# Embedding lookup with added positions: first indices on the SyncE ring, first positions on the ScalarE ring

## Chip, cores and metric

One core of a Trainium2 chip. The metric is the device time of one execution in microseconds (us), lower is better. "Span" is the time from the first to the last instruction in the trace; it is some 5 us shorter than the device time.

In lines of the profile, DVE is VectorE, POOL GpSimd, ACT ScalarE and SP SyncE; a q behind the name is the engine's sequencer, which issues transfers and waits. A ring is the queue on which one engine's transfers reach the 16 transfer (DMA) engines. A load has landed when the last of its 16 semaphore increments has arrived. GpSimd's sequence of gathers is called its row.

## The reference

```python
def reference(indices, embedding_table, position_embed):
    token_embed = embedding_table[indices]          # indices (32, 512), table (50000, 512) float32
    return (token_embed + position_embed).astype(np.float32)   # positions (512, 512)
```

16,384 rows of 2 KB are gathered (33.6 MB), added to a position and stored (33.6 MB).

## The kernel before

Each of the 128 gathers brings 128 rows (256 KB) into a slot, GpSimd issues it, VectorE adds the positions, ScalarE issues the store. Before the gathers can start, the indices of the first batch must be in SBUF. That load and the first half of the positions are issued inside Tile's part of the program, which `tc.close()` and `tc.compile()` end with barriers across all engines (line 106); everything else comes after it.

```python
    def load(out, in_, done):
        return nc.scalar.dma_start(out=out, in_=in_).then_inc(done, 16)
    # ...
    for ins in (load(idx0[:, 0, :], idx_first[:, 0, :], s_first), load_pos(0)):
        tc.no_tile_sem_insts.add(ins.ins.name)
    tc.close()
    tc.compile()                       # barriers of all engines

    load(idx0[:, 1:, :], idx_first[:, 1:, :], s_next)      # the remaining indices of batches 1 to 3
    for j in range(J):
        load(idx_raw[j * B : (j + 1) * B, :], idx_rows[:, j, :], s_raw)
    load_pos(1)

    nc.gpsimd.wait_ge(s_first, 16)
    for g, (b, k) in enumerate(order):
        if g == half:                  # the third gather
            nc.gpsimd.wait_ge(s_next, 16)
        # ...
        ins = nc.gpsimd.indirect_dma_start(
            out=slots[b % SLOTS][:, k, :], out_offset=None, in_=table,
            in_offset=bass.IndirectOffsetOnAxis(ap=where, axis=0),
        ).then_inc(s_gather[g % LANES], 16)
    # ...
    # VectorE: copy of the positions to PSUM, then one add per gather
    # ScalarE: one store per add or pair of adds
```

## Time and profile before

| what | before |
|---|---|
| time, median of the first four runs | 179.29 us (178.99 to 179.32) |
| span | 173.3 us |
| GpSimd leaves Tile's barriers | 2.25 us |
| first indices landed (last of 16 increments) | 2.33 us |
| first gather starts | 3.13 us |
| step from gather to gather | 1.251 us |
| DMA rate from 40 us on | 410 to 419 GB/s |

The prediction below shows the lines that bound this kernel. Two more are from the timeline of the start; the columns are start, duration, engine, line, operation, and in brackets the idle time before it and what ended it. The first is VectorE's first copy of the positions, the second its second add:

```profile
4.64 0.69 DVE L145 COPY pos_ps<-pos_sb 128x512 f32<-128x512 f32 x1 [4.64 <-DMA pos_sb<-in_position_embed_dram]
...
10.28 0.69 DVE L150 TENSOR_TENSOR slot<-slot,pos_ps 128x512 f32<-128x512 f32 x1 [2.19 <-DMA slot<-in_embedding_table_dram,idx]
```

The copy waits for the positions alone, the add for the second gather's data.

### The profile page before, as it was taken

The page shows a single profiled execution, that of the slowest core. Times are in us where ns is not written, and L with a number is a line of the kernel's source. Part 1 is how long each engine was busy: PE and PEld are TensorE (multiplying, and loading weights), DVE is VectorE, ACT ScalarE, POOL GpSimd, SP SyncE. Part 2 cuts the span into 40 slices and gives each one's busy share as a digit, 9 for nine tenths or more (in the row PEclk, how much of TensorE's full clock was granted, in tenths as well). Part 3 has the DMA queues.
Part 4 walks back from the last instruction along what each step waited for, and adds up shares of the span by engine and source line. Part 5 has one row for each costly group of instructions (what it writes and reads, how often), then busy time and mean ns, then how long its engine had stood idle before and what let it go on. Part 6 is the DMA issues. An engine that isn't in the chain of part 4 may idle for free.

```text
span 173.3 us, 387 instructions
## 1 busy us (share of the span) xinstructions
DVE 90.7 (52%) x133; POOL 121.4 (70%) x132
## 2 busy tenths in 40 slices
DVE  0433855545555554555555555545555555546551
POOL 2777777777777777777777777777777777777400
DMA  4899999999999999999999999999999999999997
GB/s 128 242 324 331 345 392 365 415 409 412 411 415 402 407 421 419 409 421 420 420 416 421 420 417 419 422 416 420 421 419 417 421 419 418 419 422 415 420 420 308
DMA packets 21059, 68.34 MB, mean 394 GB/s; under 512 B 3776, under 2 KB 3904, under 8 KB 21056
## 3 DMA queue, kind: packets, MB, share of 16 engines
q10 hardware_dynamic: 10816, 34.76, 49.8%
q0 software_dynamic: 10240, 33.56, 49.7%
q14 instruction: 3, 0.02, 0.0%
HBM read 34.75 MB, written 33.55 MB: 394 GB/s over the span
## 4 chain that ended last, share of the span: by engine, by line
POOL 68%; issue 23%; DMA 5%; DVE 1%; POOLq 0%
POOL slot L128 68%; DMA slot<-in_embedding_table_dram,idx_t 4%; DVE slot L150 1%; DMA idx<-in_indices_dram 1%; POOLq L123 0%
## 5 line engine op out<-in xcount | busy, mean ns | idle before, releaser
L128 POOL DMA_INDIRECT slot<-in_embedding_table_dram,idx_t x112 | 105.9, 946 | 34.1 <-issue 34.1
L150 DVE TENSOR_TENSOR slot<-slot,pos_ps 128x512 f32<-128x512 f32 x128 | 87.9, 687 | 74.9 <-issue 46.1
L128 POOL DMA_INDIRECT slot<-in_embedding_table_dram,idx x16 | 15.3, 954 | 7.3 <-issue 4.6
L145 DVE COPY pos_ps<-pos_sb 128x512 f32<-128x512 f32 x4 | 2.8, 688 | 4.6 <-DMA pos_sb<-in_position_embed_dram 4.6
L140 DVE STREAM_TRANSPOSE idx_t<-idx_raw 128x128 int32<-128x128 int32 x1 | 0.4, 399 | 0.0
L186 POOL MEMSET const-float32-0.0<- 128x1 f32 x1 | 0.1, 98 | 0.2 <-issue 0.2
L186 POOL MEMSET const-uint8-127<- 128x1 uint8 x1 | 0.1, 118 | 0.0
L186 POOL MEMSET const-bfloat16-1.0<- 128x1 bf16 x1 | 0.1, 113 | 0.0
L186 POOL MEMSET const-float32-1.0<- 128x1 f32 x1 | 0.1, 104 | 0.0
## 6 DMA issues: line engine op xcount, KB each, us to landing
out_dram<-slot ACTq DMA_DIRECT2D x60, 512.0 KB
out_dram<-slot ACTq DMA_DIRECT2D x8, 256.0 KB
slot<-in_embedding_table_dram,idx_t POOLq DMA_INDIRECT x112
pos_sb<-in_position_embed_dram ACTq DMA_DIRECT2D x2, 512.0 KB, 4.6
slot<-in_embedding_table_dram,idx POOLq DMA_INDIRECT x16
idx_raw<-in_indices_dram ACTq DMA_DIRECT2D x4, 32.0 KB
idx<-in_indices_dram ACTq DMA_DIRECT2D x1, 4.0 KB, 1.6
idx<-in_indices_dram ACTq DMA_DIRECT2D x1, 12.0 KB
```

The source lines that it names most:

```text
L128: ins = nc.gpsimd.indirect_dma_start(out=slots[b % SLOTS][:, k, :], out_offset=None, in_=table, in_offset=bass.IndirectOffsetOnAxis(ap=whe ...
L140: nc.vector.transpose(out=idx_t[:], in_=idx_raw[:].rearrange("r (q k w) -> r k q w", k=K, w=2)[:, :, :, 0],)._wait_ge(s_raw, 16 * J).then_ ...
L145: nc.vector.tensor_copy(out=pos_ps[:, k, :], in_=pos_sb[:, k, :])._wait_ge(s_pos[k // half], 16).then_inc(s_ps, 1)
L150: nc.vector.tensor_tensor(out=part, in0=part, in1=pos_ps[:, k, :], op=add)._wait_ge(s_gather[g % LANES], rounds(g)).then_inc(s_add, 1)
L186: nc = _bacc.Bacc("TRN2", target_bir_lowering=False, num_devices=1)
```

## The change

ScalarE issues both early loads one after the other, which keeps it, and so the barrier, busy until 1.6 us. The change gives the index load to SyncE, so that the two issues run side by side.

```diff
-    def load(out, in_, done):
-        return nc.scalar.dma_start(out=out, in_=in_).then_inc(done, 16)
+    def load(out, in_, done, engine=nc.scalar):
+        return engine.dma_start(out=out, in_=in_).then_inc(done, 16)
 ...
-    for ins in (load(idx0[:, 0, :], idx_first[:, 0, :], s_first), load_pos(0)):
+    for ins in (
+        load(idx0[:, 0, :], idx_first[:, 0, :], s_first, engine=nc.sync),
+        load_pos(0),
+    ):
         tc.no_tile_sem_insts.add(ins.ins.name)
```

## The prediction

> **What bounds the kernel now.** I read the page first, then the waits, then the timeline of the first microseconds, the chain of waits (whole, and in windows at both ends), and last the DMA view of the first three microseconds.
>
> The page, parts 4 and 5:
>
> ```profile
> DVE 90.7 (52%) x133; POOL 121.4 (70%) x132
> POOL 68%; issue 23%; DMA 5%; DVE 1%; POOLq 0%
> L128 POOL DMA_INDIRECT slot<-in_embedding_table_dram,idx_t x112 | 105.9, 946 | 34.1 <-issue 34.1
> ```
>
> The chain that ended last is GpSimd: 128 gathers, each 946 ns of descriptor making, plus a gap "issue" before each. The list of waits says how large that gap is and whether the gathers ever wait for data:
>
> ```profile
> POOL slot L128 <- issue: 38.7, 127, 0.3
> POOL slot L128 <- DMA idx<-in_indices_dram: 2.7, 1, 2.7
> ```
>
> 127 gaps of 0.30 us, and one wait on data: the first gather's, for the first indices. So one gather comes every 0.946 + 0.305 = 1.25 us and nothing stops the row. The timeline has the first gather at 3.13 and the last at 162.06: 158.93 us for 127 steps, 1.2514 each. Each step brings 256 KB in and, later, sends 256 KB out: 524,288 B in 1.2514 us is 419 GB/s.
>
> The same figure is the DMA rate of the steady part, so the DMA could be the bound instead. Cutting the span into stretches gives:
>
> ```profile
> 12.00:14.00 2.00, 1.37 (x3) 1.68 (x2) 1.00 1.00 326
> 80.00:120.00 40.00, 21.84 (x32) 30.25 (x33) 1.00 1.03 419
> ```
>
> The fifth number on is the DMA share, then GB/s: the transfer engines are full from about 12 us. But pairing each gather with its add on the timeline (start to start) gives 3.7 us for the first gather, 5.8 for the second, 6.7 at the eleventh, 7.3 at the 30th and 7.4 at the 66th, the 102nd and the last. If the transfers were slower than GpSimd, this delay would keep growing by the difference at each step; it is flat from 40 us on. I therefore read GpSimd as the pacer and the DMA as just keeping up. The whole time is then a sum: first gather's start 3.13 + 127 x 1.2514 = 162.06; + 7.47 to its add = 169.54; + 0.69 for the add = 170.22; + some 3.0 for the last store and the clearing of semaphores = 173.3, the span. The timed runs have 179.27, so 6 us lie outside the span.
>
> Only the first term, 3.13, can be touched by this change. Its make-up, from the timeline and the chain in a window of the start:
>
> ```profile
> 0.74 0.38 ACTq L95 DMA_DIRECT2D idx<-in_indices_dram  x1
> 1.15 0.46 ACTq L95 DMA_DIRECT2D pos_sb<-in_position_embed_dram  x1
> 2.36 0.39 ACTq L95 DMA_DIRECT2D idx<-in_indices_dram  x1
> ```
>
> ```profile
> 0.74 1.60 DMA idx<-in_indices_dram
> 2.33 0.80 issue
> 3.13 1.08 POOL slot L128
> ```
>
> The indices are issued at 0.74, land at 2.33, and 0.80 us pass before the first gather shows. Beside this runs a second path: Tile closes its part with barriers (line 106) which all engines must reach. ACT reaches them only after its two issues:
>
> ```profile
> L106 ACTq DRAIN  x2: 8/80/151, 1.6 to 2.0; - x2
> ...
> L106 POOLq EVENT_SEMAPHORE  x2: 17/17/17, 2.2 to 2.2; - x2
> ```
>
> (the second line is the same line of source in the window from 2.1 to 3 us). In the record of single instructions ACT's drain starts at 1.645, GpSimd collects the five engines at 1.83, goes through a second round and leaves at 2.25, 0.08 us before the last of the sixteen index increments (2.33). So two paths reach the first gather almost together.
>
> **What the Trainium skill says.** "DMA: Bandwidth & Descriptors", section "Issuing engines are not separate DMA queues": transfers from all engines run on the same 16 DMA engines, and issuing from several saves only sequencer time. The trace has that time: 0.38 and 0.46 us on ACT's sequencer. The same page, "Queues, rings and completion order": SyncE and ScalarE own one ring each, each DMA engine takes turns between rings at packet granularity, and a semaphore increment lands only after every earlier write of that engine across its queues. The trace before has one hardware ring (q10) in use and can't show it. "Perfetto Trace Analysis", "DMA Instruction — HWDGE (DVE, Sync)": the descriptor generator is shared and is locked by one sequencer at a time. The trace before has no two issues at once, so doesn't show that either. The same page, "DMA Instruction — SWDGE (GPSIMD)": on GpSimd an instruction waits in a queue after decoding and the recorded time is that of the software that writes descriptors, so part of the 0.80 us is not in any record.
>
> **The change part by part.** Removed: ACT's first issue, 0.38 us plus the 0.03 to the next, 0.41 in all. Added: one issue on SyncE, which has nothing to do but the barrier. Moved: the positions' issue, from 1.15 to 0.74 (ACT leaves the opening barrier there).
>
> Step 1, the index landing. SyncE leaves the opening barrier 5 ns before ACT, so its issue starts at about 0.73 too. Same 0.38 issue, same 1.60 to landing: 2.33. The saving is nil, since the index load was already first on its own ring.
>
> Step 2, the positions. Before, they were issued at 1.15 and landed 3.5 later (the tile's own answer), and the first copy on VectorE began at 4.64. All 0.41 earlier: 4.23. VectorE's next step, the first add, waits for the first gather until 6.81, so the 0.41 us are idle time exchanged for idle time: 0.
>
> Step 3, the barrier. ACT's drain moves from 1.645 to about 1.23 (SyncE done at 0.73 + 0.38 = 1.11 is no later), hence GpSimd's exit from 2.25 to 1.84. The other loads on ACT (remaining indices, from 2.36) move to 1.95, the second positions from 4.73 to 4.32. The third gather needs the remaining indices only at 5.76, and they had landed by 4.73: 0.
>
> Step 4, contention. In the DMA view of the first 3 us (40 slices of 0.075 us), this row is the transfer engines' busy share:
>
> ```profile
> DMA  0000000000000000000000023300018934558999
> ```
>
> Index packets move from 1.73 to 2.0 and the first position packets from 2.24. Positions issued 0.41 earlier would start at 1.83, in the middle of the indices. Index packets took 9 ns each, position packets (4096 B) 159 ns at best and up to 0.69 us. Each engine has 8 index packets; as the engines' index completions are spread from 1.80 to 1.99 and the positions would sweep the engines in the same order about 0.1 behind, I estimate that most index packets stay ahead, and charge 0 to 0.4 us, 0.1 as the middle.
>
> Step 5, the 0.80. If it counts from the landing, the first gather moves to 3.13 + 0.1 = 3.23. If a part of it is GpSimd's own way from the barrier to the gather, it starts 0.41 earlier and the first gather can come as early as 2.72. VectorE's first copy came 0.02 after its last increment, and gathers with no wait follow in 0.30, so 0.80 after a landing is long; that speaks for the second. I give it one in three.
>
> Sum: 0.65 x (+0.1) + 0.35 x (-0.35) = -0.06 us. Everything after the first gather keeps its pace, so the time moves by the same: 179.27 - 0.06, about **179.2 us**.
>
> **Rivals.** (a) The barrier frees the first gather: 2.72 instead of 3.13, 178.9 us. For it: the odd 0.80 and the near tie of 2.25 and 2.33. Against it: the chain names the index DMA, and the landing itself isn't earlier. (b) The positions delay the indices: either ACT gets the generator first (the indices wait 0.4) or 4096 B packets stand between the 32 B ones, or a completion waits behind a position write. For it: the overlap worked out in step 4, which the old order on one ring avoided. Against it: SyncE is 5 ns ahead and its issue is 0.07 shorter. One to several packets of 0.16 to 0.5 us make +0.3 to +0.8: 179.6 to 180.1 us. (c) The DMA is the true bound and swallows a shift of GpSimd; then the earlier positions fill a hole in the transfers (their share is 0.72 from 4 to 6 us) and up to 0.3 us are won: 179.0. The flat 7.4 us speaks against it. (d) A second hardware ring costs something outside the span. No number here bears on it; I leave it a small chance of a microsecond or more.
>
> **Range and chances.** The first gather can move between -0.41 and about +0.8. The runs before lie between 178.99 and 179.32, so the median carries 0.2 either way. That makes 178.6 to 180.2; I cut the far end of (b) a little and take 178.5 to 180.0. Two per cent is 3.6 us, more than the whole 3.13 us that the change can touch going down, and four times the worst contention going up: within 2% at 0.98, one per cent each way.
>
> **What would show it.** Right: the issue of the indices on SyncE's queue at 0.73 to 0.76, positions on ACT's at 0.74; position landing near 4.2; the barrier on GpSimd ending at 1.8 to 1.9; gathers still every 1.25 us and 7.4 us to the add late in the run; the span moved by as much as the first gather's start. Step 1 is wrong if the indices land later than 2.5 (then b); step 5 is wrong if the first gather comes before 3.0 with the landing unmoved (then a). The pacer reading is wrong if the first gather's start moves and the end doesn't follow (then c), and if the span stays and the timed runs move, it is (d). The whole is wrong if the gathers' period changes: nothing here should do that.

## The result, and the profile after

The changed kernel took 178.51 us (median of four runs, 178.26 to 178.83); the kernel before 179.29 us in the same rounds. The ratio is 0.9962, 95% interval 0.9943 to 0.9981. Ratios in this document are the mean time of one kernel's fast runs over that of the other's of the same set, so not quite the ratio of the medians quoted. In all sets but this first one they come out of the listed runs only if the first run of each list is left out (that of the run under test is the profiled execution); means and differences in the text are over all listed runs.

The page of the changed kernel says that nothing happened to the bulk of the work (parts 4 and 5), and that 144 packets now go over a second hardware ring, q1 (part 3; packets, MB, share):

```profile
q10 hardware_dynamic: 10672, 34.75, 49.6%
q1 hardware_dynamic: 144, 0.00, 0.0%
...
POOL 65%; issue 25%; DMA 5%; DVE 3%
...
L131 POOL DMA_INDIRECT slot<-in_embedding_table_dram,idx_t x112 | 106.0, 947 | 34.1 <-issue 34.1
```

The list of waits of the changed kernel gives the same row of gathers: 127 gaps of 0.3 us and one wait on data at the start, 2.5 us now:

```profile
POOL slot L131 <- issue: 38.7, 127, 0.3
POOL slot L131 <- DMA idx<-in_indices_dram: 2.5, 1, 2.5
```

So the difference lies in the first microseconds. The timeline there:

```profile
0.74 0.40 ACTq L95 DMA_DIRECT2D pos_sb<-in_position_embed_dram  x1
0.74 0.37 SPq L95 DMA_DIRECT2D idx<-in_indices_dram  x1
1.90 0.40 ACTq L95 DMA_DIRECT2D idx<-in_indices_dram  x1
...
3.99 0.69 DVE L148 COPY pos_ps<-pos_sb 128x512 f32<-128x512 f32 x1 [3.99 <-DMA pos_sb<-in_position_embed_dram]
...
8.78 0.69 DVE L153 TENSOR_TENSOR slot<-slot,pos_ps 128x512 f32<-128x512 f32 x1 [0.80 <-DMA slot<-in_embedding_table_dram,idx]
```

The two issues are side by side at 0.74, ScalarE's next one comes at 1.90 instead of 2.36, the positions are there 0.65 us earlier, and the second add comes 1.5 us earlier. The chain of waits in the window from 0 to 9 us (start, duration, what):

```profile
0.74 1.97 DMA idx<-in_indices_dram
2.71 0.27 issue
2.98 1.08 POOL slot L131
```

Before it was 1.60, then 0.80, then the gather at 3.13. The indices now take 0.37 us longer to land, and yet the gather comes 0.15 us earlier, because the piece that follows the landing shrank from 0.80 to 0.27. GpSimd's last two steps of the barrier, in the window from 1.6 to 3 us, are earlier (2.2 before; count, ns, first and last start):

```profile
L109 POOLq EVENT_SEMAPHORE  x2: 17/17/17, 1.7 to 1.8; - x2
```

The second of them ends at 1.79, before at 2.25. The DMA view of the first 3 us shows why the landing is later. Each digit is the busy share of the transfer engines in 0.075 us:

```profile
DMA  0000000000000000000000029795499999949999
```

Before there was a hole between the indices (1.73 to 2.0 us) and the positions (from 2.24). Now the positions' packets begin at 1.81, while the last of the index packets are sent at 2.27 instead of 1.98, and the sixteen 4 B packets that make the load's increments start from 1.99 to 2.44 instead of 1.80 to 1.99 (both from the packet records of the traces).

That accounts for 0.15 us at the first gather, and even this isn't there at the end: the last gather of the two traces starts at the same 162.06 and both spans are 173.3 us. The other 0.6 us of the measured 0.78 is in none of these lines, so the first question was whether it is there at all.

### The profile page after: what moved, and what is told of

It reads as the page before. It is cut to its first block, busy times and chain, and to the rows that moved or that the text cites. A ratio compares the mean times of both kernels' runs of the same rounds, so it can differ in the third digit from the quotient of the medians.

```text
span 173.3 us, 387 instructions
## 1 busy us (share of the span) xinstructions
DVE 90.6 (52%) x133; POOL 121.5 (70%) x132
## 4 chain that ended last, share of the span: by engine, by line
POOL 65%; issue 25%; DMA 5%; DVE 3%
POOL slot L131 65%; DMA slot<-in_embedding_table_dram,idx_t 4%; DVE slot L153 3%; DMA idx<-in_indices_dram 1%
```

## The experiments

Two theories stood at the start. **T, two gates:** the first gather comes at the later of two times, a fixed time after GpSimd leaves the barrier, and 0.27 us after the indices land; the end follows GpSimd's row. **D:** something else wins, either the second ring outside the span, or the earlier transfers. A second question runs through all of them: does GpSimd's row set the end, or the transfers, which have no slack to see?

### after_again: the changed kernel once more

No edit. 

> The changed kernel once more, to size the 0.78 us. Theory T (two gates): the first gather comes at the later of barrier exit + up to 0.88 us and index landing + 0.27 us, and the rest of the kernel follows it; then the gain is the 0.15 us by which the first gather moved in the trace, ratio 0.9992, and the 0.9962 was mostly chance. Rival D (outside the span or another place): the ratio is again near 0.996 (0.994 to 0.998) while the first gather is only 0.15 us earlier.

Measured: 178.63 us against 178.56, ratio 1.000 (0.9969 to 1.003), first gather at 3.06 us. The 0.996 did not come back.

### before_again: the kernel before against itself

No edit. 

> The kernel before against itself: ratio 1.000. Both theories say the same; how far the ratio is from 1 says how small a difference the other runs can show. If it is off by more than 0.2%, differences of 0.2% are not to be explained.

Measured: 178.53 us, ratio 0.9993 (0.9967 to 1.002), first gather at 3.13. The half width of the interval is 0.27%, or 0.5 us: a difference of 0.15 us can be read in a trace, but not in these times. One source of the spread is visible: leaving out the first step, which is longer, the mean step from gather to gather was 1.2504 us in the first trace of this kernel and 1.2531 in this one, which makes 0.34 us over 126 steps.

### after_third: the changed kernel a third time

No edit. 

> The changed kernel a third time, to pool with the two earlier sets (ratios 0.9962 and 1.000). If there is a gain of the size of the first set, 0.994 to 0.998; if it is the 0.1 to 0.2 us of the first gather or nothing, 0.998 to 1.002.

Measured: 178.45 us against 178.54, ratio 0.9988 (0.9954 to 1.0023), first gather at 2.95. In the two repeats the means differ by 0.15 and 0.14 us (178.60 and 178.75; 178.42 and 178.56). In the first set the difference was 0.69, and most of it came from the other side: the four runs of the kernel before averaged 179.22, while its 11 runs in each later set averaged 178.75, 178.56 and 178.58. The changed kernel averaged 178.53, 178.60 and 178.42. Why the first four runs of before were slow isn't settled; the traced execution of that kernel took 177.92 us, 1.07 below the fastest of them. The gain in the repeats is of the order of the first gather's shift (0.07 and 0.18 us), but it hangs on single runs: without the first run of each list, as in the ratios, it is 0.01 and 0.21 us. Both intervals include 1, so a gain in time is not shown.

### idx_alone_act: only the indices in Tile's part, on the old ring

```diff
-    for ins in (load(idx0[:, 0, :], idx_first[:, 0, :], s_first), load_pos(0)):
+    for ins in (load(idx0[:, 0, :], idx_first[:, 0, :], s_first),):
         tc.no_tile_sem_insts.add(ins.ins.name)
     tc.close()
     tc.compile()
+    load_pos(0)
     load(idx0[:, 1:, :], idx_first[:, 1:, :], s_next)
```

> Only the first indices in Tile's part, on the ScalarE ring as before; the first positions right after the barrier, on the same ring. No second ring, no rival transfer for the indices. Theory T: barrier exit at about 1.7 us as in the changed kernel, indices landing at 2.33 as before, first gather at 2.33 + 0.27 = 2.60, so 0.53 before the kernel before, and the time 0.4 to 0.5 us below it (ratio 0.9975). If the 0.80 us counted from the landing instead, the first gather stays at 3.13. Rival D (the second ring or the early positions make the gain): ratio 1.000, since neither is there; positions land near 5.2 instead of 4.6.

Measured: 178.74 us, ratio 0.9987 (0.9954 to 1.0019). The landing is where it was (2.33), the barrier opens at 1.77 instead of 2.25, and the first gather comes at 2.65: the 0.80 us before it did not count from the landing. But the time did not move. The timeline of this run says what took the gain:

```profile
2.65 1.08 POOL L129 DMA_INDIRECT slot<-in_embedding_table_dram,idx  x1 [2.20 <-DMA idx<-in_indices_dram]
...
4.04 0.94 POOL L129 DMA_INDIRECT slot<-in_embedding_table_dram,idx  x1 [0.30 <-issue]
...
5.71 0.95 POOL L129 DMA_INDIRECT slot<-in_embedding_table_dram,idx  x1 [0.73 <-DMA idx<-in_indices_dram]
```

The third gather waits for the remaining indices, which now stand behind the positions: a step of 1.67 instead of 1.25 us, 0.42 of the 0.48 won. A new wait took the place of the old one, and I had not seen it coming.

### idx_alone_sp: the same on the SyncE ring

```diff
-    for ins in (load(idx0[:, 0, :], idx_first[:, 0, :], s_first),):
+    for ins in (load(idx0[:, 0, :], idx_first[:, 0, :], s_first, nc.sync),):
```

> As the run before, but the first indices go on the SyncE ring; positions again after the barrier. Theory T: the same first gather, about 2.60, and the same time as that run within 0.2 us. Rival D, if the second ring itself is worth something outside the span: 0.5 us or more below the run with the ScalarE ring, with the same span.

Measured: 178.95 us, ratio 1.0009 (0.9983 to 1.0035); landing 2.33, first gather 2.67, again a long third step (1.49 us). The second ring brings no gain by itself, and no cost that these runs could show: the device time minus the span was 5.2 us here and 5.0 with the old ring. The mean times of the two lie 0.42 us apart, not within the 0.2 that I expected, with overlapping intervals. In the trace, the adds lag behind the gathers by 8.1 us late in the run, against 7.6 with the old ring; this comes back below.

### rest_first: the new wait taken away

From the run before, with the remaining indices ahead of the positions:

```diff
     tc.compile()
-    load_pos(0)
     load(idx0[:, 1:, :], idx_first[:, 1:, :], s_next)
+    load_pos(0)
```

> As the run with the indices alone on the SyncE ring, but after the barrier the remaining indices go ahead of the first positions, so the third gather doesn't have to wait for them. First gather at about 2.65, steps of 1.25 us from there with no long one, so the last gather some 0.45 us before the kernel before's. If GpSimd's row alone sets the end, the time is 0.4 us below before (ratio 0.9975). If the transfers decide, then the later positions (landing near 5.5 instead of 4.6) take back what the earlier gather gives: first add not before 6.8, delay from gather to add near 8 instead of 7.4 in the steady part, ratio 1.000 within 0.2%.

Measured: 178.13 us against 178.38, ratio 0.997 (0.9938 to 1.0002); the spans average 172.95 us over 6 runs against 173.56 over 11. The chain of the start, from 0 to 6 us:

```profile
0.74 1.57 DMA idx<-in_indices_dram
2.31 0.36 issue
2.67 1.08 POOL slot L131
3.75 0.30 issue
4.06 0.95 POOL slot L131
```

No step is long, the last gather starts at 161.67, 0.39 before the kernel before's, and the delay from gather to add in the steady part is 7.2 us, not the 8 that the transfer theory wanted, although the positions land only at 6.41 and the first add comes at 7.64 instead of 6.81. The mean time is 0.57 us lower. So the end followed GpSimd's row, and the later positions took nothing back. But of the 0.69 us by which the last add is earlier, only 0.39 is the row; 0.30 is a shorter delay to the add, which no theory here had foreseen. This is the best of the versions tried, but its interval just touches 1, so that it beats both kernels is likely rather than shown.

### both_sp: both early loads on the SyncE ring

```diff
-    for ins in (load(idx0[:, 0, :], idx_first[:, 0, :], s_first), load_pos(0)):
+    for ins in (
+        load(idx0[:, 0, :], idx_first[:, 0, :], s_first, nc.sync),
+        load_pos(0, nc.sync),
+    ):
```

> Both of Tile's loads on the SyncE ring, indices first, nothing on ScalarE before the barrier: the kernel before with the other ring. One ring in order: indices land at 2.33; SyncE now holds the barrier until about 1.8, GpSimd leaves at 2.25. If the barrier gates the first gather, it comes at 3.1 to 3.15 as before, whichever engine holds it; if SyncE's ring is what matters, it comes earlier.

Measured: one run, 178.97 us. GpSimd leaves the barrier at 2.27, the indices land at 2.44, the first gather starts at 3.15. It does not matter which engine holds the barrier up; the first gather waits for it.

### swap: the two rings exchanged

```diff
-        load(idx0[:, 0, :], idx_first[:, 0, :], s_first, engine=nc.sync),
-        load_pos(0),
+        load(idx0[:, 0, :], idx_first[:, 0, :], s_first),
+        load_pos(0, nc.sync),
```

> The changed kernel with the two rings exchanged: indices on the ScalarE ring, positions on the SyncE ring, both in Tile's part. If the indices' 0.38 us of delay comes from the positions being issued 5 ns sooner and taking a shared generator, then now the indices are first: they land at about 2.35, the first gather at 2.62. If it comes from the transfer engines taking turns between two rings, the indices land at 2.6 to 2.8 again and the first gather at 2.9 to 3.05. The time: within 0.3% of before either way.

Measured: 180.21 us against 178.54, ratio 1.0089 (1.0044 to 1.0134). Neither landing that I had expected came, and the time left the 0.3% that I had allowed. The chain of this run:

```profile
0.74 3.70 DMA idx<-in_indices_dram
4.44 0.27 issue
4.71 1.08 POOL slot L131
```

and its DMA view of the first 3 us:

```profile
DMA  0000000000000000000000099850529919594949
```

Nothing but the assignment of rings changed: the issues still start 5 ns apart (0.736 on ScalarE, 0.741 on SyncE) and the barrier opens at 1.79 as in the changed kernel. In both traces, what was issued on SyncE reached the transfer engines first. Here these were the positions, at 1.77; in the changed kernel the indices, at 1.72, with the positions 0.09 behind. The first index packet of this run starts at 2.12, and the sixteen increments come between 3.83 and 4.44. With a lead of 0.09 us the indices pay 0.38 us, 0.35 us behind they pay 2.1.

### idx_second_sp: the indices well behind the positions, on the SyncE ring

```diff
     for ins in (
+        load(idx0[:, 1:, :], idx_first[:, 1:, :], s_next, engine=nc.sync),
         load(idx0[:, 0, :], idx_first[:, 0, :], s_first, engine=nc.sync),
         load_pos(0),
     ):
 ...
-    load(idx0[:, 1:, :], idx_first[:, 1:, :], s_next)
```

> The changed kernel with the SyncE ring carrying the remaining indices first and the first indices second, so that they start 0.4 us after the positions. If SyncE's ring is simply served ahead of ScalarE's, they land 0.4 to 0.6 us later than in the changed kernel, at 3.1 to 3.3. If the rings take turns packet by packet, the 32 B packets now sit between 4096 B ones all the way: landing at about 4 or later, as in the exchanged rings (4.44), and the first gather 0.27 after it.

Measured: one run, 181.06 us; the first indices land at 5.26, 4.04 after their issue at 1.22, and the first gather comes at 5.53. So the SyncE ring is not simply served ahead of the other. That the packets in front are what counts fits, but is not shown by this run alone, since the first indices also stood behind the 384 packets of the remaining indices on their own ring. One thing remains open: the positions, issued at 0.74 as before, sent only a few packets before 2.6 us (the eighth began at 2.80, against 1.88 in the changed kernel). That they stood behind the descriptors of SyncE's larger load is a guess.

### eager: a try at a faster one

The second positions right after the barrier on ScalarE, the remaining index loads on SyncE, to fill the hole in the transfers between 4 and 6 us.

```diff
-    load(idx0[:, 1:, :], idx_first[:, 1:, :], s_next)
-    for j in range(J):
-        load(idx_raw[j * B : (j + 1) * B, :], idx_rows[:, j, :], s_raw)
-    load_pos(1)
+    load_pos(1)
+    load(idx0[:, 1:, :], idx_first[:, 1:, :], s_next, engine=nc.sync)
+    for j in range(J):
+        load(idx_raw[j * B : (j + 1) * B, :], idx_rows[:, j, :], s_raw, engine=nc.sync)
```

> A try at a faster one: the changed kernel with the second positions issued on the ScalarE ring right after the barrier (1.9 instead of 4.3 us) and the remaining indices on the SyncE ring. First gather unchanged at 2.95 to 3.05. If the transfers decide the end, filling the hole between 4 and 6 us is worth 0.3 to 0.8 us of time. If GpSimd's row decides, nothing; if the early 512 KB get in the way of the first gathers, the first adds come later and nothing is won either, ratio 1.000.

Measured: 180.58 us, ratio 1.0111 (1.0081 to 1.014). The timeline of this run:

```profile
4.01 1.08 POOL L131 DMA_INDIRECT slot<-in_embedding_table_dram,idx  x1 [3.56 <-DMA idx<-in_indices_dram]
...
7.49 0.94 POOL L131 DMA_INDIRECT slot<-in_embedding_table_dram,idx  x1 [1.14 <-DMA idx<-in_indices_dram]
```

Both index loads ran into position traffic. The remaining indices hold the third gather for 1.14 us instead of 0.30. And the first indices landed at 3.74 instead of 2.71, although the loads of Tile's part are those of the changed kernel: the first 64 of their 128 packets had started by 1.92 (1.83 in the changed kernel), but the sixteen 4 B packets of the increments started only from 2.63 to 3.41. The lead over the positions was 0.08 us here and 0.07 to 0.09 in the three traces of the changed kernel, where the index landing was 2.71, 2.78 and 2.67. What made this trace differ is not shown. The loads added after the barrier were issued at 1.91, and a load's first packet never came sooner than 0.97 us after its issue here, so they can hardly have held up the packets before 2.8. That it is a close race, which this run lost, is a guess.

### extra_dma: 1 MB more to move, nothing more for GpSimd

```diff
+    for n in range(2):
+        nc.sync.wait_ge(s_add, 48 + 16 * n)
+        if n:
+            nc.sync.wait_ge(s_pad, 16 * n)
+        nc.sync.dma_start(
+            out=pad[:], in_=table[n * 256 : (n + 1) * 256].rearrange("(p k) d -> p (k d)", k=2)
+        ).then_inc(s_pad, 16)
```

> The kernel before with two extra loads of 512 KB from SyncE in the middle of the run, whose data nobody uses: 1.05 MB more for the transfer engines, nothing more for GpSimd. If the transfers bound the steady part: 1,048,576 B at 419 GB/s = 2.5 us more, ratio 1.014. If GpSimd paces it and the transfers only keep up: under 0.5 us, and the extra shows only as a delay from gather to add that rises by 2.5 us and then falls back.

Measured: 180.23 us against 178.54, ratio 1.0099 (1.0053 to 1.0146); the spans average 176.12 against 173.59, 2.53 us more. The windows of this run from 60 us on (the last two numbers are the DMA share and GB/s), and the last gather and the last add on its timeline:

```profile
60.00:80.00 20.00, 10.20 (x16) 15.12 (x17) 1.00 1.03 418
80.00:100.00 20.00, 10.17 (x16) 15.12 (x17) 1.00 1.03 419
...
140.00:160.00 20.00, 11.32 (x17) 15.12 (x17) 1.00 1.03 420
```

```profile
162.32 0.94 POOL L137 DMA_INDIRECT slot<-in_embedding_table_dram,idx_t  x1 [0.30 <-issue]
...
172.05 0.69 DVE L159 TENSOR_TENSOR slot<-slot,pos_ps 128x512 f32<-128x512 f32 x1 [0.41 <-issue]
```

GpSimd's row ends where it did; the delay from gather to add rose from 7.35 us (48th gather) to 9.74 (84th) and was still 9.73 at the last. The rate did not go above 420 GB/s, so the backlog was never worked off. The transfers have no slack that 80 us could show: what is added to them is added to the span. In the timed runs it came to 1.74 us, in the spans to 2.53; I can't say why the two differ.

### slow_gpsimd: GpSimd's row made longer in the middle

```diff
+        if g % 4 == 3 and 32 <= g < 112:
+            nc.gpsimd.memset(pad[:, (g - 32) // 4, :], 0.0)
```

> The kernel before with twenty small memsets between gathers 32 and 112 on GpSimd: some 0.1 to 0.3 us each in its row, so the last gather comes 2 to 6 us later; nothing more for the transfers. If GpSimd paces the run: the time rises by as much as the last gather moved. If the transfers bound it: the delay from gather to add falls from 7.4 us by the same amount and the time stays within 0.5 us, as long as that delay stays above the 3.7 us of an unhindered gather.

Measured: 188.09 us against 178.54, ratio 1.0535. In the trace the last gather starts at 175.60, 13.5 us later than before, and its add comes 7.36 us after it. While the row was slow, the delay fell from about 7.9 us to as little as 4.1, and grew again when the steps were back at 1.25 us. The end follows the row. But the dose was not what I had planned: the first twelve memsets cost only some 0.02 us each, less than wanted; seven between 108 and 151 us lengthened their steps to 2.1 to 3.5 us, though each lasts 0.15 to 0.18, and the last again cost 0.02. The seven make 10.1 of the 13.5 us; steps without a memset in the same stretch also grew, most of them to 1.4. Why, I don't know, and the mean time rose by 9.6 us where the span rose by 13.1. I take from it the direction alone.

### The two gates over all runs

Fourteen traces give one rule; its two constants, 0.88 and 0.27, were taken from the first traces of the two kernels, so the other twelve test it. "Gate 1" is GpSimd's exit from the barrier plus 0.88 us, "gate 2" the index landing plus 0.27; the later one should be the first gather.

| kernel | barrier exit | landing | gate 1 | gate 2 | first gather |
|---|---|---|---|---|---|
| before | 2.25 | 2.33 | **3.13** | 2.60 | 3.13 |
| before_again | 2.25 | 2.33 | **3.13** | 2.60 | 3.13 |
| extra_dma | 2.26 | 2.34 | **3.13** | 2.61 | 3.14 |
| slow_gpsimd | 2.25 | 2.34 | **3.13** | 2.61 | 3.13 |
| both_sp | 2.27 | 2.44 | **3.15** | 2.70 | 3.15 |
| idx_alone_act | 1.77 | 2.33 | **2.65** | 2.60 | 2.65 |
| idx_alone_sp | 1.79 | 2.33 | **2.67** | 2.60 | 2.67 |
| rest_first | 1.79 | 2.31 | **2.67** | 2.58 | 2.67 |
| after | 1.79 | 2.71 | 2.67 | **2.98** | 2.98 |
| after_again | 1.79 | 2.78 | 2.67 | **3.05** | 3.06 |
| after_third | 1.79 | 2.67 | 2.67 | **2.95** | 2.95 |
| eager | 1.81 | 3.74 | 2.69 | **4.01** | 4.01 |
| swap | 1.79 | 4.44 | 2.67 | **4.71** | 4.71 |
| idx_second_sp | 2.38 | 5.26 | 3.26 | **5.53** | 5.53 |

And the end follows GpSimd's row. "Row" is the shift of the first gather against 3.13 plus what long steps add; "time" is the difference of the mean times within the same set.

| kernel | row, us | time, us |
|---|---|---|
| rest_first | -0.46 | -0.57 |
| idx_alone_sp | -0.46 + 0.24 = -0.22 | +0.23 |
| after, three sets | -0.15, -0.07, -0.18 | -0.69, -0.15, -0.14 |
| idx_alone_act | -0.48 + 0.42 = -0.06 | -0.19 |
| before_again | 0 | -0.12 |
| swap | +1.58 | +1.64 |
| eager | +0.88 + 0.84 = +1.72 | +1.87 |

Apart from the first set of the changed kernel, all are within half a microsecond, which is the width that the kernel shows against itself.

The row is not the only term of the end: the delay from gather to add is the other. Over the last 63 gathers its median was 7.4 us in both traces of the kernel before, 7.5, 7.25 and 7.6 in those of the changed one, 7.2 in rest_first, 8.1 in idx_alone_sp and 8.3 in both_sp. So in idx_alone_sp the last gather starts 0.23 us earlier than before (161.83) and the last add 0.47 later (170.01), and its mean time is 0.23 higher. This delay differs between traces of one kernel by as much as the gain that was sought. Its median over the 40th to 65th gathers lies within 0.2 us of that over the last 63 in every trace but extra_dma and slow_gpsimd, and extra_dma shows that what is added to it stays. What sets it in the first 40 us was not tested.

## Why the prediction was right or wrong, point by point

**The measure of the whole.** 179.2 was forecast, 178.51 came out in the first set, 0.01 us inside the lower edge of the range; that it lay inside is luck, since the repeats gave 178.63 and 178.45, one on each side of that edge. The effect was forecast as -0.06 us; the three traces give -0.15, -0.07 and -0.18 at the first gather, and the two repeats -0.15 and -0.14 in time, not resolved from zero. The rest of the first set's 0.78 us did not repeat.

**What bounds the kernel.** GpSimd as the pacer held: rest_first, swap, eager and slow_gpsimd moved the row, and the time went with it. "The DMA as just keeping up" held more literally than meant: extra_dma shows no slack at all. The flat 7.4 us, from which I argued, is a backlog that does not shrink while the row keeps its pace, so it does not show spare bandwidth. Two readings were off: the 66th gather's delay is 7.3, not 7.4, which changes nothing, and the "6 us outside the span" takes time and span from different executions; the traced one took 177.92 us, 4.6 more than its span. One step of 1.25 us is what GpSimd needs to make a gather's descriptors and also what the transfers need for 512 KB. Hence rival (c) was wrong in its conclusion, that the transfers swallow a shift, and right in its premise, that they are full.

**Step 1, the landing.** Wrong. "SyncE leaves the opening barrier 5 ns before ACT, so its issue starts at about 0.73 too" was the reasoning; it did leave first, but its issue began 5 ns after ScalarE's (0.743 and 0.738). The landing moved from 2.33 to 2.71. The 5 ns did not decide this: in swap the indices' issue began 5 ns first, and they landed at 4.44.

**Step 2, the positions.** Right in that they gain nothing, too small in size: the first copy moved by 0.65 us, not 0.41, because the issue moved by 0.41 and the load itself was quicker.

**Step 3, the barrier.** Right: 1.79 measured, 1.84 forecast. The expected 1.95 for ScalarE's next load was 1.90.

**Step 4, contention.** The mechanism was right and its size was off: 0.1 us was charged and 0.34 to 0.45 measured. "Most index packets stay ahead" held for the data: the 64th of the 128 packets started at 1.83 to 1.84 us in all three traces of the changed kernel, as before, and the last at 2.27, 2.06 and 2.07 instead of 1.98. What the step left out are the sixteen 4 B packets of the increments, which the landing waits for. They started between 1.80 and 1.99 us before, between 1.99 and 2.44 in the changed kernel (2.11 and 2.42, 2.00 and 2.33 in its repeats), among position packets of 0.16 us or more; the last increment arrived 0.28 to 0.36 us after the last of them, before as after. Rival (b) had this, as "a completion waits behind a position write"; whether they waited for the write or for a turn, the records don't show. The Trainium skill, "DMA: Bandwidth & Descriptors", section "Queues, rings and completion order", has the rings served in turns, packet by packet; the traces agree with that, since 32 B packets that were through by 1.98 alone are still being sent at 2.06 to 2.27 beside position packets, and when they start behind (swap), the first increment arrives only at 3.83. The term that failed is the 0.1 us of this step.

**Step 5, the 0.80.** I gave one chance in three to the barrier. It was the barrier, with 0.88 us from its exit to the first gather, and the landing needs only 0.27. The near tie of 2.25 and 2.33 hid which of the two was waited for; the chain of waits put it down to the indices because they came last by 0.08 us.

**The sum.** The two misses are of opposite sign. The barrier alone would have brought 0.46 us (rest_first has it), the later landing took back 0.31 of them: gate 2 at 2.98 instead of gate 1 at 2.67. The weighted sum of -0.06 was near the result by luck: it weighed a later landing alone against an earlier barrier alone, where in fact both came and the later gate counted.

**The rivals.** (a) happened and (b) happened, in the same run. (b) where it ruled alone, in swap, cost 1.6 us, twice the worst that I had given it. (d), a cost of the second ring outside the span, did not show.

## What to carry to other kernels

When two waits end within a tenth of a microsecond of each other, a profile names the later one, and the time after it may belong to the other; move one of them alone and see. A small load that the critical path waits for should go alone, or well ahead of big ones: beside a 512 KB load on another ring it lost 0.34 to 0.45 us in three traces and 1.4 in a fourth (eager) with a lead of 0.07 to 0.09 us, and 2.1 us when it was 0.35 behind. Before a difference of a few tenths of a per cent is explained, run the kernel against itself: here that alone showed an interval of half a microsecond to either side. And a shift at the start reaches the end only together with whatever else differs: here the delay from gather to add varied as much.

## What the Trainium skill lacked or had wrong

- "DMA: Bandwidth & Descriptors", "Issuing engines are not separate DMA queues", says that issuing from several engines saves only the sequencer's time. It gives no size for the other side: which ring carries which load changed the landing of a 4 KB load from 1.97 us (changed kernel) to 3.70 us (rings exchanged), and alone it took 1.57 to 1.60.
- No page read for this case has the time from a barrier to the first indirect gather: 0.88 us after GpSimd's exit in eight traces, against 0.27 us after a semaphore that comes later, in six.
- "Perfetto Trace Analysis", "DMA Instruction — HWDGE (DVE, Sync)", has issues wait for a shared generator inside the profiled time. Two issues 5 ns apart took 0.40 us (positions) and 0.37 (indices); without another beside it, the first positions' issue took 0.34 to 0.51 and the indices' on SyncE 0.37, so no such wait can be read from the issue's duration here.
- No page read says why memsets of 0.15 to 0.18 us cost a row of gathers 0.02 us each twelve times and then 0.9 to 2.2 us each (slow_gpsimd, seven memsets from 108 to 151 us), nor why device times rise by less than the spans (9.6 against 13.1 us there, 1.74 against 2.53 in extra_dma).
